# Layer one's modulation weights in 1 MB transfers, the negative maxima of four tiles in one copy, new transfer costs in the planner

## The chip, the cores and the metric

The kernel runs on one core of a Trainium2 chip. The metric is the device time of one execution in microseconds (us), lower being better; three runs of the kernel before gave a median of 1363.16 us (1362.76 to 1366.52).

The names used below: PE is TensorE, which multiplies matrices; PEld is its loading of weights; DVE is VectorE; ACT is ScalarE; POOL is GpSimd; SP is SyncE, which here issues nearly every transfer between memories (DMA). Each engine works through its own list of instructions in order, and waits at one whose inputs are not there yet.

## The reference

Two layers of a diffusion backbone over 1024 tokens of width 1024, with 256 context tokens. Each layer computes a shift, a scale and a gate from a conditioning vector (the modulation, `silu(c) @ w_mod[i] + b_mod[i]`), normalises and modulates the tokens, mixes them and adds the gated result. Layer zero's mixer is grouped-query attention (16 query heads, 4 key heads, width 64) over tokens and context; layer one's is attention in a neighbourhood of 8 rows by 16 columns plus the context.

```python
for i in range(DEPTH):
    mod_x = (silu_c @ w_mod[i] + b_mod[i])[:, None, :]
    mod_c = silu_cc @ w_mod[i] + b_mod[i]
    sh_x, sc_x, g_x = jnp.split(mod_x, 3, axis=-1)
    hx = rms_norm(x, norm_g[i]) * (1.0 + sc_x) + sh_x
    ...
    if i % N_MIXERS == 0:
        yx, yc = gqa_axial_mixer(hx, hc, ...)
    else:
        yx, yc = neighbourhood_mixer(hx, hc, ...)
    x = x + g_x * yx
return rms_norm(x, final_norm_g)
```

Inside layer zero's mixer, for each block of queries: `s = q @ k_all * scale`, `p = softmax(s)`, `o = p @ v_all`.

## The kernel before

**Tiles and stages.** The 1024 tokens are eight tiles of 128, the context two more. Matrix products run in 16-bit floats with each operand split into a high and a low part. The stages follow each other on PE: loading, normalisation and the key/value projection (to about 96 us of the trace); layer zero's attention over eight head pairs `u`, with the projections of the next pair and the modulation blocks beside it (to about 650 us); the output projection and the second normalisation (to about 810 us); layer one's attention, again eight pairs (to about 1290 us), and the last output projection.

**Layer zero's attention.** For each head pair `u` the tiles form three groups (`pt`): four tiles, four tiles, and the two of the context. `a_proj` projects queries (`pa`, L946), normalises and rotates them into `q16`, and a transposing DMA (L963) puts them into `q1`, whose lower half a copy (L965) puts into `q2`. `mgen` computes all scores once for their maximum alone: matmuls `pm` (L976) and `pmc` (L982), each followed by a maximum on DVE. `rows` reduces these maxima over a group, negates them into a 128x128 tile `zmax` (L1001), transposes that by DMA into `zt` (L1002), and copies its rows into partition 64 of `q2` (L1006, L1008), so that the product of 65 rows of `q2` and `k2` (L1184) already holds the score less its maximum. Then `a_att` forms transposed scores `st` (L1183, L1184), takes the exponential twice on ACT (`ph` L1168, `pf` L1170), splits off the low part on POOL (`pl`, L1045), and multiplies by the values (`pv`, L1051 to L1053).

For the first six pairs (`QH`) only one head of the two goes that way. The other head goes through `q_att`: scores `qs` (L1116 on `q1`, L1117 on `q2`) with queries on the partitions, a maximum on DVE (L1119), the exponentials, and transposing DMAs of 2048 columns (`qpt`, L1130; `qct`, L1139) ahead of the product with the values (`qpv`, L1104). In these pairs `q2` is `[128, 4 tiles, 2 heads, 128]`, and only head 0 of each tile gets a row of maxima: four rows apart in memory, copied one by one (L1006). In the last two pairs, and for the context, both heads get rows, in one copy (L1008).

`pm`, `pmc` and `qs` share two buffers of the matmul memory (tag `mx`), `st` has two of its own.

**The modulation blocks.** `mod_block` runs eight times within layer zero's attention: two for layer zero's gate, six for layer one. Each loads 512 columns of `w_mod` in two halves of four row tiles into `wg`, which has one buffer (L602, one 256 KB transfer per row tile), multiplies them (L610), and writes the result to memory.

**What sets the order.** The code emits work in a hand-written time line (`timeline`, by places such as `u + 0.2`). Then `Planner` takes all instructions, computes which depends on which, and simulates the five engines with `cost` (busy time, and time until the result is there), five times over with due times from the pass before; the best order it finds is fixed on each engine. For its dependencies `box` takes an access as the range from its first to its last element in each partition. For a DMA, `cost` returns the time to issue it on SP and the time that it holds the DMA engines.

Of the kernel before, what the change touches and what calls it, by code (L numbers as in the profile page):

```python
# [13 lines left out]
F16 = mybir.dt.float16  # L14
# [7 lines left out]
P = 128  # L22
D = 1024
KT = D // P
# [22 lines left out]
class Planner:  # L47
# [42 lines left out]
    def cost(self, x, rd, wr):  # L90

        k, e = type(x).__name__, self.ENG[x.engine.name]
        outs = [a for a in x.outs if hasattr(a, "bass_ap")]
        ins = [a for a in x.ins if hasattr(a, "bass_ap")]
        n = max([self.elems(a) for a in outs + ins] or [1])
        psum = any(str(getattr(a.bass_ap.tensor, "space", "")) == "PSUM" for a in ins)
        if e == "PE":
            f32 = ins[0].dtype == mybir.dt.float32
            cols = self.elems(outs[0])
            if outs[0].bass_ap.tensor.name.startswith("warm"):  # L100
                return 130.0, 170.0
            passes = (2 if x.is_transpose else 4) if f32 else 1
            if f32 and any("idf" in a.bass_ap.tensor.name for a in ins):
                passes = 2
            if not f32 and cols <= 65:
                return 30.0 if cols == 65 else 34.0, 170.0
            return max(cols * passes / 2.4 + 3.0, 29.0), 170.0
        if k == "InstDmaTransposeAnt":
            m = 1
            for s, c in list(ins[0].ap):  # L110
                m *= c
            return 1340.0, m / 128 * 23.4 / 16
        if k == "InstDMACopy":
            m = 1
            for s, c in list(outs[0].ap):
                m *= c
            run = [self.run(a) for a in (outs[0], ins[0])]
            ro = min(min(run), 1024) * 4
            return (470.0 if len(list(outs[0].ap)) < 3 else 600.0), m * 4 / ro * (11 + ro * 0.0432) / 16
        if e == "ACT":  # L120
            ptr = sum(1 for a in ins[1:] if self.elems(a) == 1)
            o = n / 1.2 + (50 if psum else 85) + (100, 100, 200)[ptr] * (ptr > 0) + (93 if len(outs) > 1 else 0)
            return o, 110.0
        if e == "DVE":
            two = len([a for a in ins if self.elems(a) > 2]) > 1
            rate = 0.96
            if not psum and not two and k in ("InstTensorCopy", "InstTensorScalarPtr"):
                rate = 3.84 if all(a.dtype != mybir.dt.float32 for a in ins + outs) else 1.92
            return n / rate + 70, 82.0
        if e == "POOL":  # L130
            if k == "InstTensorTensor":
                if getattr(x, "op", None) == mybir.AluOpType.pow:
                    return 980.0 if n > 1 else 560.0, 30.0
                return 150 + n * (1.95 if any(a.dtype != mybir.dt.float32 for a in ins) else 2.1), 40.0
            return 60 + n, 40.0
        return 50.0, 50.0
# [365 lines left out]
def trunk_kernel(ctx, tc, x, cx, cc, norm_g, ng_row, b_cols, sel_c, w_mod, w_mod0, b_mod, a_qz, a_kv, a_qg, a_kg, a_w_out,  # L502
                 b_in, rpb, b_w_out, fin_g, cos_t, sin_t, mask_q, out):
    nc = tc.nc
    V, S, G, T, DM = nc.vector, nc.scalar, nc.gpsimd, nc.tensor, nc.sync
# [6 lines left out]
    def ps_pj(name, dt=F32, shape=(P, 512)):  # L512
        return psum.tile(list(shape), dt, name=name, tag="pj", bufs=2)
# [79 lines left out]
    def mod_block(pool, l, c0):  # L593

        nm = f"{l}{c0}"
        r = c0 // D
        row = pool.tile([P, P], F32, name="mrow" + nm, tag="mrow", bufs=1)
        for hf in range(2):
            wm = pool.tile([P, KT // 2, 512], F32, name=f"wg{nm}{hf}", tag="wg", bufs=1)
            for i in range(KT // 2):  # L600
                kt = hf * KT // 2 + i
                DM.dma_start(wm[:, i], w_mod[l, kt * P:(kt + 1) * P, c0:c0 + 512])  # L602
                yield 1.0
            if hf:
                brow = com.tile([P, 512], F32, name="brow" + nm, tag="stage", bufs=4)[0:1]
                DM.dma_start(brow, b_mod[l:l + 1, c0:c0 + 512])
            ps = ps_pj(f"pmg{nm}{hf}", shape=(P, 2, P))
            for i in range(KT // 2):
                for j in range(4):
                    T.matmul(ps[32 * j:32 * j + 32, 0], s2[:, hf * KT // 2 + i, :], wm[:, i, j * P:(j + 1) * P],  # L610
                             start=i == 0, stop=not hf and i == KT // 2 - 1)
            if hf:
                for j in range(4):
                    T.matmul(ps[32 * j:32 * j + 32, 0], twos, brow[:, j * P:(j + 1) * P], start=False, stop=True)
            if not hf:
                V.tensor_copy(row, ps[:, 0])
            else:
                V.tensor_tensor(row, ps[:, 0], row, op=ALU.add)
        if r == 1:
            gr = pool.tile([P, P], F32, name="gr" + nm, tag="gr", bufs=1)  # L620
            g0 = ng_row[l:l + 1, c0 - D:c0 - D + 1]
            DM.dma_start(gr, bass.AP(g0.tensor, g0.offset, [[P, 4], [0, 32], [1, P]]))
            V.tensor_scalar(row, row, 0.5, 1.0, op0=ALU.mult, op1=ALU.add)
            V.tensor_tensor(row, row, gr, op=ALU.mult)
        else:
            V.tensor_scalar_mul(row, row, 0.5 / WS if r == 2 else 0.5)
        for v in range(2):
            dst = gate_d[l, v, c0 - 2 * D:c0 - 2 * D + 512] if r == 2 else mod_d[r, v, c0 % D:c0 % D + 512]
            DM.dma_start(dst.rearrange("(j c) -> j c", c=P), row[v:P:32])
        yield 1.0  # L630
# [292 lines left out]
    def a_proj(u, at):  # L923
# [62 lines left out]
        def rows(pts):  # L986

            zm = zmax[nrow[0] % len(zmax)]
            nrow[0] += 1
            zf = aq.tile([P, 16], F32, name=f"zf{u}{pts[0]}", tag="zf", bufs=2)  # L990
            zt = aq.tile([P, P], F16, name=f"zt{u}{pts[0]}", tag="zt", bufs=2)
            c0, outs = 0, []
            for pt_ in pts:
                mxs, n = pairs[(u, pt_)][3], PTN[pt_]
                hs = (0,) if pt_ < 2 and u in QH else (0, 1)
                zv = zf[:, c0:c0 + n * len(hs)].rearrange("p (t h) -> p t h", h=len(hs))
                for i in hs:
                    V.tensor_reduce(zv[:, :, i], mxs[i] if pt_ < 2 else mxs[i][:, 0:n, 2:3], axis=AX.X, op=ALU.max)
                outs.append((c0, n, len(hs), pairs[(u, pt_)][1]))
                c0 += n * len(hs)  # L1000
            V.tensor_scalar(zm[:, 0:c0], zf[:, 0:c0], -1.0, CSH, op0=ALU.mult, op1=ALU.add)  # L1001
            DM.dma_start_transpose(zt, zm)  # L1002
            for c, n, h, q2 in outs:
                for t in range(n) if h == 1 else (None,):
                    if h == 1:
                        DM.dma_start(q2[64:65, t, 0, :], zt[c + t:c + t + 1])  # L1006
                    else:
                        DM.dma_start(q2[64:65], zt[c:c + n * h])  # L1008
            yield 200

        items = []
        for b in range(NT // 2):
            m = (1100 if u in QH else 2200) if b < 4 else 440
            if u == 0:
                v, w, vp, vm, mw = FIRST[b]
            else:
                v = at + 0.2 * b
                w, vp, vm, mw = 0.2, v + 0.29, v + 0.31, 0.2 * m / (1100 if u in QH else 2200)
            items.append((mm(b), v, v + w, 5120))
            items.append((post(b), vp, vp + 0.01, 220))  # L1020
            items.append((mgen(b), vm, vm + mw, m))
            if b in (1, 4):
                items.append((rows((0,) if b == 1 else (1, 2)), vm + mw + 0.01, vm + mw + 0.02, 400))
# [216 lines left out]
    for n, m in enumerate(mods):  # L1240
        items.append((mod_block(aq, *m), 0.1 + 0.9 * n, 0.1 + 0.9 * (n + 1), 9.0))
# [417 lines left out]
```

## Time and profile before

| | |
|---|---|
| median of three runs | 1363.16 us (1362.76 to 1366.52) |
| profiled execution, its own time | 1365.58 us |
| its span, first to last instruction | 1363.8 us |
| granted PE clock | 0.999 |
| DMA packets, bytes | 426,959, 198.23 MB, mean 145 GB/s |
| hardware queue of SP | 426,216 packets, 195.98 MB, 65.3% of the engines' time |

A row of the profile names line, engine, operation, what is written and read (`out<-in`, buffer numbers left out), the shape and the count. Windows are in us from the start of the span. `SPq` is SP's queue, whose issuing of transfers is not counted as an engine's work. Matmuls overlap each other, and their ends are modelled.

### The profile page before, as it was taken

How to read it: one execution, taken by the hardware profiler on the slowest of the kernel's cores; microseconds unless marked ns; L12 is line 12 of the kernel's file. 1: busy time of each engine (PE TensorE's matmuls, PEld its weight loads, DVE VectorE, ACT ScalarE, POOL GpSimd, SP SyncE). 2: the span in 40 equal slices, each digit the busy share in tenths (PEclk: the TensorE clock that was granted, in tenths of full speed). 3: DMA queues.
4: the chain of work that ended last, by engine and by line, in shares of the span. 5: the costliest groups of instructions: out<-in, count | busy, mean ns of one | idle time of the engine just before them, and what ended most of it. 6: DMA issues, size and time to landing. Idle time of an engine off the chain costs nothing.

```text
span 1363.8 us, 34709 instructions
## 1 busy us (share of the span) xinstructions
PE 1329.9 (98%) x13183; PEld 927.6 (68%) x13183; DVE 1003.1 (74%) x2647; ACT 910.2 (67%) x2186; POOL 664.7 (49%) x855
## 2 busy tenths in 40 slices
PE   9999999999999999999999999999999999999897
PEld 6457777777777777776554486777768686867543
DVE  5788788878788789887276846777776867777743
ACT  3653788888787876878632437777776777786711
POOL 2573787777778775788743201312222222332332
PEclk9999999999999999999999999999999999999999
DMA  9652577878789777847066725666576656677932
GB/s 352 186 162 76 108 145 156 154 161 166 149 152 169 146 150 138 172 145 210 10 171 175 178 80 120 125 132 138 117 153 110 156 96 146 113 159 141 194 101 102
DMA packets 426959, 198.23 MB, mean 145 GB/s; under 512 B 382560, under 2 KB 389664, under 8 KB 426792
## 3 DMA queue, kind: packets, MB, share of 16 engines
q1 hardware_dynamic: 426216, 195.98, 65.3%
q8 instruction: 103, 1.69, 0.5%
q14 instruction: 64, 0.52, 0.1%
q10 hardware_dynamic: 576, 0.03, 0.0%
HBM read 90.51 MB, written 15.22 MB: 78 GB/s over the span
## 4 chain that ended last, share of the span: by engine, by line
PE 68%; DVE 11%; ACT 9%; DMA 5%; POOL 3%; issue 3%; SPq 1%; DVEq 0%; POOLq 0%; ACTq 0%
PE pa L946 11%; PE pb L1360 9%; PE pvz L1393 9%; PE poa L1275 7%; PE pob L1566 6%; PE st L1183 2%; PE st L1184 2%; PE pkv L817 2%; ACT bpf L1464 2%; PE pm L976 2%; PE bpv L1473 1%; PE pv L1052 1%; PE qpv L1104 1%; PE pv L1053 1%; PE pv L1051 1%
## 5 line engine op out<-in xcount | busy, mean ns | idle before, releaser
L1045 POOL TENSOR_TENSOR pl<-pf,ph 128x256 f16<-128x256 f32 x340 | 234.1, 714 | 58.2 <-ACT pf L1170 44.5
L1045 POOL TENSOR_TENSOR bph<-bpf,bph 128x256 f16<-128x256 f32 (+1 forms) x128 | 99.9, 790 | 319.5 <-ACT bpf L1464 256.3
L946 PE MATMUL pa<-wa,x 128*128 128x256 f16 x1536 | 213.4, 272 | 0.1
L1360 PE MATMUL pb<-hb_hi,wb 128*128 128x512 f16 (+1 forms) x640 | 193.3, 358 | 1.4 <-DVE bk L1379 1.0
L1393 PE MATMUL pvz<-wb,hb_hi 128*128 128x256 f16 x1024 | 175.4, 273 | 0.6 <-DVE bk L1379 0.3
L946 PEld LDWEIGHTS <-x 128*128 128x128 f16 x1536 | 143.2, 97 | 35.7 <-issue 1.3
L1168 ACT ACTIVATE ph<-st 128x512 f16<-128x512 f32 x200 | 119.1, 604 | 60.7 <-PE st L1184 50.0
L1360 PEld LDWEIGHTS <-wb 128*128 128x128 f16 x960 | 92.7, 98 | 72.5 <-issue 2.9
L1393 PE MATMUL pvz<-wb,hb_lo 128*128 128x256 f16 x512 | 139.6, 273 | 0.0
L1170 ACT ACTIVATE pf<-st 128x512 f32<-128x512 f32 x200 | 119.3, 609 | 1.7 <-POOL pl L1045 1.6
L977 DVE TENSOR_REDUCE mxp<-pm 128x1 f32<-128x512 f32 x160 | 107.9, 684 | 13.7 <-PE pm L976 12.3
L1045 POOL TENSOR_TENSOR qpp<-qpf,qpp 128x512 f16<-128x512 f32 x84 | 97.9, 1186 | 38.4 <-ACT qpf L1127 32.2
L1360 PE MATMUL pb<-hb_lo,wb 128*128 128x512 f16 (+1 forms) x320 | 114.4, 358 | 0.0
L1393 PEld LDWEIGHTS <-hb_hi 128*128 128x128 f16 x1024 | 97.1, 98 | 24.2 <-DVE bk L1379 1.1
L1051 PE MATMUL pv<-v,ph 128*128 128x65 f16 x800 | 104.0, 193 | 0.2 <-ACT ph L1168 0.2
L1052 PE MATMUL pv<-v,ph 128*128 128x64 f16 x800 | 104.0, 195 | 0.0
L1053 PE MATMUL pv<-v,pl 128*128 128x65 f16 x800 | 101.4, 192 | 0.5 <-POOL pl L1045 0.5
L1566 PE MATMUL pob<-wob,ob 128*128 128x512 f16 x384 | 86.7, 379 | 2.6 <-DVE bmx L1444 0.9
L1051 PEld LDWEIGHTS <-ph 128*128 128x128 f16 x800 | 75.8, 97 | 19.0 <-ACT ph L1168 0.7
L1462 ACT ACTIVATE bph<-bpf,bnx 128x384 f16<-128x384 f32 (+1 forms) x128 | 68.7, 582 | 27.2 <-DVE bnx L1454 27.1
L1052 PEld LDWEIGHTS <-ph 128*128 128x128 f16 x800 | 75.5, 97 | 12.6
L1053 PEld LDWEIGHTS <-pl 128*128 128x128 f16 x800 | 76.1, 99 | 10.5 <-POOL pl L1045 1.6
(272 smaller groups left out, 3812.1 us busy)
## 6 DMA issues: line engine op xcount, KB each, us to landing
wg<-in_w_mod SPq DMA_DIRECT2D x64, 256.0 KB
wsb<-in_b_in SPq DMA_DIRECT2D x64, 256.0 KB
wm<-in_w_mod SPq DMA_DIRECT2D x16, 512.0 KB
wsa<-in_a_qz SPq DMA_DIRECT2D x32, 256.0 KB
xstage<-in_x SPq DMA_DIRECT2D x8, 512.0 KB
wsoa<-in_a_w_out SPq DMA_DIRECT2D x16, 256.0 KB
x<-in_x SPq DMA_DIRECT2D x8, 512.0 KB
x_d<-x SPq DMA_DIRECT2D x8, 512.0 KB
```

The lines of the kernel that those rows point to most:

```text
L946: T.matmul(ps[:, :, i, :], hA(a, kt, t), wt[w][:, kt, :], start=n == 0, stop=n == 3 * KT - 1)
L977: V.tensor_reduce(mxs[i][:, t, ch:ch + 1], pm, axis=AX.X, op=ALU.max)
L1045: G.tensor_tensor(lo[:, c], p32[:, c], hi[:, c], op=ALU.subtract)
L1051: T.matmul(pv[:, t, :], hi[:, c], v[:, 0:65], start=first and t == 0, stop=False)
L1052: T.matmul(pv[:, t, 0:HD], hi[:, c], v[:, 65:129], start=False, stop=False)
L1053: T.matmul(pv[:, t, :], lo[:, c], v[:, 0:65], start=False, stop=last and t == n - 1)
L1168: S.activation(ph, st, AF.Exp)
L1170: S.activation(p32, st, AF.Exp)
L1275: T.matmul(ps, lhs(a, kt), w[b][:, kt, :], start=n == 0, stop=n == 3 * KT - 1)
L1360: T.matmul(ps[:, 0:n].rearrange("p (t q) -> p t q", q=P), wt[a][:, kt, which * P:(which + 1) * P], hb[b][:, c0 // P:(c0 + n) // P, kt], st ...
L1393: T.matmul(ps[:, :, j, :], hb[a][:, t, kt], wt[w][:, kt, 256:512], start=m == 0, stop=m == 3 * KT - 1)
L1566: T.matmul(ps, ob[kt][:, t // 4, a, c], wout["b"][hf][b][:, kt, :], start=n == 0, stop=n == 3 * KT - 1)
```

## The change

Three edits. The four loads of a `wg` half become one transfer of 1 MB, through a view of `w_mod` with the row tile as an inner dimension; the step that `timeline` counts for it is the same in sum. The copies of negative maxima become one per group for every pair: for the first six pairs it writes four places of `q2` from four rows of `zt`. And the planner's costs change: a transposing DMA of 2048 columns takes 1900 ns to issue in place of 1340, and a copy's bytes follow the type, two per element for 16-bit floats in place of four throughout, with runs counted in bytes up to 4096.

```diff
         if k == "InstDmaTransposeAnt":
 ...
-            return 1340.0, m / 128 * 23.4 / 16
+            return (1900.0 if m == 2048 * P else 1340.0), m / 128 * 23.4 / 16
         if k == "InstDMACopy":
 ...
-            ro = min(min(run), 1024) * 4
-            return (470.0 if len(list(outs[0].ap)) < 3 else 600.0), m * 4 / ro * (11 + ro * 0.0432) / 16
+            by = 2 if outs[0].dtype == F16 else 4
+            ro = min(min(run) * by, 4096)
+            return (470.0 if len(list(outs[0].ap)) < 3 else 600.0), m * by / ro * (11 + ro * 0.0432) / 16
 ...
             wm = pool.tile([P, KT // 2, 512], F32, name=f"wg{nm}{hf}", tag="wg", bufs=1)
-            for i in range(KT // 2):
-                kt = hf * KT // 2 + i
-                DM.dma_start(wm[:, i], w_mod[l, kt * P:(kt + 1) * P, c0:c0 + 512])
-                yield 1.0
+            r0 = hf * KT // 2 * P
+            DM.dma_start(wm, w_mod[l, r0:r0 + KT // 2 * P, c0:c0 + 512].rearrange("(k p) c -> p k c", p=P))
+            yield 4.0
 ...
             for c, n, h, q2 in outs:
-                for t in range(n) if h == 1 else (None,):
-                    if h == 1:
-                        DM.dma_start(q2[64:65, t, 0, :], zt[c + t:c + t + 1])
-                    else:
-                        DM.dma_start(q2[64:65], zt[c:c + n * h])
+                DM.dma_start(q2[64:65, :, 0, :] if h == 1 else q2[64:65], zt[c:c + n * h])
```

SP has 84 transfers fewer: 48 loads of `wg` and 36 row copies. No other engine has an instruction more or less, but the planner's order of all of them is new; on PE it is nearly the old one again from layer one's first projection on (282 of 9,988 rows stand elsewhere). From L603 to L1000 a line keeps its number; those after L1008 stand four lines higher in the new kernel (L1117 is L1113 there, L1184 is L1180).

First piece, PE, where the first head pair's scores begin. In the names the first digit is the pair, the second the group; `q1` and `q2` are the queries, `pm02` a tile of maxima, `qs00` the scores of `q_att`, `st00` those of `a_att`. Before:

```order
L976 LDWEIGHTS q101_1466
L976 MATMUL pm02000_1627<-k1_128,q101_1466 128x512
L1116 LDWEIGHTS q100_1314
L1116 MATMUL qs0000_1673<-k1_128,q100_1314 128x512
L1117 LDWEIGHTS q200_1315
L1117 MATMUL qs0000_1673<-k2_129,q200_1315 128x512
L1116 LDWEIGHTS q100_1314
L1116 MATMUL qs0001_1698<-k1_128,q100_1314 128x512
L1117 LDWEIGHTS q200_1315
L1117 MATMUL qs0001_1698<-k2_129,q200_1315 128x512
```

Now, at the same place, and fourteen projection matmuls later:

```order
L976 LDWEIGHTS q101_1466
L976 MATMUL pm02000_1624<-k1_128,q101_1466 128x512
L1112 LDWEIGHTS q100_1314
L1112 MATMUL qs0000_1670<-k1_128,q100_1314 128x512
L1112 LDWEIGHTS q100_1314
L1112 MATMUL qs0001_1695<-k1_128,q100_1314 128x512
```

```order
L1180 LDWEIGHTS k2_129
L1180 MATMUL st0000_1654<-q200_1315,k2_129 128x512
L1113 LDWEIGHTS q200_1315
L1113 MATMUL qs0000_1670<-k2_129,q200_1315 128x512
L1113 LDWEIGHTS q200_1315
L1113 MATMUL qs0001_1695<-k2_129,q200_1315 128x512
```

The second half of each `qs` product, which read `q2` ahead of the row copies, now stands behind the first `st` that needs them, and the two `qs` tiles stay open meanwhile.

Second piece, SP, the same group's transpose and copies (`zt00`, `q200`). Before:

```order
L963 DMA_TRANSPOSE q101_1466<-q16q02_1554 128x4x128
L965 DMA q201_1467<-q101_1466 64x512
L1002 DMA_TRANSPOSE zt00_1593<-zmax0_1303 128x128
L963 DMA_TRANSPOSE q101_1466<-q16q03_1643 128x4x128
L1006 DMA q200_1315<-zt00_1593 1x16x8 x4
L606 DMA brow02048_3006<-in_b_mod 1x512
L965 DMA q201_1467<-q101_1466 64x512
```

Now:

```order
L963 DMA_TRANSPOSE q101_1466<-q16q02_1554 128x4x128
L1002 DMA_TRANSPOSE zt00_1593<-zmax0_1303 128x128
L965 DMA q201_1467<-q101_1466 64x512
L1004 DMA q200_1315<-zt00_1593 1x4x128
L606 DMA brow02048_2991<-in_b_mod 1x512
L963 DMA_TRANSPOSE q101_1466<-q16q03_1640 128x4x128
```

Four copies are one, the transpose of the maxima has moved ahead of a copy of queries, and a transpose of queries has moved behind.

Third piece, SP, the second group of pair 3 (`zt31`, copies into `q231` and, for the context, `q232`) beside a load of modulation weights (`wg1512`, second half). Before:

```order
L1002 DMA_TRANSPOSE zt31_6319<-zmax1_1304 128x128
L1062 DMA_TRANSPOSE oa2_5295<-ol21_5987 128x8x128
L602 DMA wg15121_6368<-in_w_mod 128x512
L1006 DMA q231_5173<-zt31_6319 1x16x8 x4
L1008 DMA q232_5746<-zt31_6319 1x4x128
L965 DMA q240_6118<-q140_6117 64x512
L1087 DMA oa_d_1299<-oa2_5295 128x2048
L1130 DMA_TRANSPOSE qpt301_6291<-qpp301_6286 128x16x128
L602 DMA wg15121_6368<-in_w_mod 128x512 x3
```

Now:

```order
L1002 DMA_TRANSPOSE zt31_6277<-zmax1_1304 128x128
L963 DMA_TRANSPOSE q140_6077<-q16q40_6298 128x4x128
L873 DMA wsa61_8352<-in_a_qz 128x512
L602 DMA wg15121_6323<-in_w_mod 128x4x512
L1004 DMA q231_5140<-zt31_6277 1x4x128
L1004 DMA q232_5707<-zt31_6277 1x4x128
L1058 DMA_TRANSPOSE oa2_5261<-ol21_5947 128x8x128
```

One of the four loads stood ahead of the copies; now the whole megabyte does.

## The prediction

> **What bounds the kernel now.** I read the page's busy shares and slices first.
>
> ```profile
> span 1363.8 us, 34709 instructions
> PE 1329.9 (98%) x13183; PEld 927.6 (68%) x13183; DVE 1003.1 (74%) x2647; ACT 910.2 (67%) x2186; POOL 664.7 (49%) x855
> PEclk9999999999999999999999999999999999999999
> GB/s 352 186 162 76 108 145 156 154 161 166 149 152 169 146 150 138 172 145 210 10 171 175 178 80 120 125 132 138 117 153 110 156 96 146 113 159 141 194 101 102
> ```
>
> TensorE (PE) is busy 98% of the span at full clock; 1363.8 - 1329.9 leaves 33.9 us idle. The change takes no matmul away, so it can only move waits. Next, the windows view by stage (the columns are the stretch, its length, then busy time and instruction count of each engine, clock, share of the DMA engines, GB/s).
>
> ```profile
> 0.00:96.00 96.00, 90.92 (x624) 52.17 (x625) 72.62 (x160) 52.53 (x105) 49.49 (x77) 1.00 0.72 241
> 96.00:650.00 554.00, 543.09 (x6786) 412.33 (x6784) 456.39 (x1238) 423.17 (x874) 402.08 (x511) 1.00 0.73 149
> 810.00:1210.00 400.00, 398.86 (x3672) 292.62 (x3670) 292.79 (x853) 294.83 (x860) 98.62 (x138) 1.00 0.65 130
> 1210.00:1290.00 80.00, 72.69 (x682) 51.80 (x681) 60.49 (x185) 63.47 (x195) 28.41 (x35) 1.00 0.79 156
> ```
>
> The edited lines run in the second row, layer zero's attention: idle there 554.0 - 543.1 = 10.9 us. What ended that idle time is the waits view of PE for this stretch (the longest of its rows; total, times, longest):
>
> ```profile
> PE st L1184 <- DMA q<-zt: 3.4, 3, 2.5
> PE st L1183 <- ACT pf L1170: 1.6, 4, 0.7
> PE qs L1116 <- DVE mxp L977: 1.3, 3, 0.5
> PE pmc L982 <- DVE mxp L977: 0.7, 2, 0.5
> PE pm L976 <- DMA q<-q16q: 0.7, 2, 0.5
> PE qpv L1104 <- DMA qpt<-qpp: 0.6, 1, 0.6
> PE qs L1116 <- DVE qmx L1119: 0.6, 2, 0.4
> PE pm L976 <- DVE mxp L977: 0.5, 2, 0.3
> ```
>
> DMA waits are 3.4 + 0.7 + 0.6 = 4.7 us, waits for VectorE (DVE) about 4.2 us with the smaller rows, the rest ScalarE and POOL. No row names `wg`, the modulation weights: PE never waits for the transfers that the first edit merges. The idle column hides a little: a 512-wide matmul is drawn 0.38 us long but the next starts 0.22 us after it (rows further down), so each wait costs some 0.16 us more than it shows.
>
> **What the edits take off SyncE's queue.** This is one line's view each (duration in ns: min/median/max):
>
> ```profile
> L602 SPq DMA_DIRECT2D wg<-in_w_mod x64: 327/454/1955, 102.9 to 618.6; - x64
> L1006 SPq DMA_DIRECT2D q<-zt x48: 506/587/1556, 127.5 to 501.4; - x48
> L1008 SPq DMA_DIRECT2D q<-zt x12: 605/662/729, 157.7 to 648.1; - x12
> L1130 SPq DMA_TRANSPOSE qpt<-qpp x48: 1511/1900/4736, 139.1 to 557.0; - x48
> SPq L1130 <- POOL pl L1045: 47.9, 22, 5.0
> ```
>
> Row copies: 48 x 0.587 = 28.2 us become 12 x 0.662 = 7.9 us (L1008 has the merged form already), so 20 us less issuing. Weights: 64 x 0.454 = 29.1 us become 16 issues of a 1 MB form that no row has; the nearest are one 256 KB issue at its shortest, 0.33 us, and four of them at the median, 1.8 us; I take 0.6, nearer the single one, since most of a row's length beyond 0.33 us is the queue's state, so 9.6 us and 19 us less. The 39 us come out of a queue that in this stretch waits for POOL 47.9 us in its first row alone: **off the path, worth 0 by themselves**. What shortens is a chain: the fourth row copy is issued 3 x 0.587 = 1.76 us after the first, and `st` needs all four. The planner's new 1.90 us for a 2048-column transpose is the median of L1130, so its plan fits these 60 instructions better; that too acts only through the order.
>
> **The chain of the negative maxima in the new order.** The last maximum matmul (`pm`, `pmc`), DVE's reductions, the transpose `zt`, the copies into row 64 of `q2`, then `st`. For the first head pair, from the timelines of PE and SyncE:
>
> ```profile
> 121.40 0.38 PE L982 MATMUL pmc<-k,q 128*128 128x256 f16 x2
> 121.61 0.27 PE L946 MATMUL pa<-wa,xc_hi 128*128 128x256 f16 x1
> 123.77 1.15 SPq L1002 DMA_TRANSPOSE zt<-zmax  x1
> 127.46 2.49 SPq L1006 DMA_DIRECT2D q<-zt  x4
> 131.25 0.60 PE L1184 MATMUL st<-q,k 65*128 65x512 f16 x2
> ```
>
> From the end of `pmc` (121.8, where DVE can start) to the transpose 2.0 us, to the copies 3.7, and `st` came at 131.25 without a wait. For the last pair, and another place where a copy was waited for (timeline of PE, chain of waits):
>
> ```profile
> 634.95 0.60 PE L982 MATMUL pmc<-k,q 128*128 128x256 f16 x4
> 635.54 0.19 PE L1053 MATMUL pv<-v,pl 128*128 128x65 f16 x1
> 635.57 0.19 PE L1051 MATMUL pv<-v,ph 128*128 128x65 f16 x1
> 639.79 7.53 DMA zt<-zmax
> 647.34 3.37 DMA q<-zt
> 650.75 0.39 PE st L1184
> 327.89 1.73 DMA q<-zt
> 350.83 0.38 PE L982 MATMUL pmc<-k,q 128*128 128x256 f16 x2
> 354.77 1.18 SPq L1002 DMA_TRANSPOSE zt<-zmax  x1
> ```
>
> (the last two rows, of the timelines, are those of pair 3's second half)
>
> A copy lands 1.73 to 3.4 us after its issue begins. With one copy the chain is at the least 2.0 + 3.7 + 1.7 = 7.4 us, up to 9.1 with the slow landing. Now the order: between the last maximum and the first `st` of that tile group stand matmuls of 0.109 us (256 wide), 0.216 us (512 wide) and 0.03 us (64 or 65 wide; starts in the rows above and below). First pair: before 61 of 256 and 10 of 512, 8.8 us; now 47 and 4, 6.0 us. The planner took the saved time and more. So PE waits 1.4 to 3.1 us here, I take 1.7. The same count gives 13.2 to 9.1 us for pair 2's second half and 13.7 to 8.2 for pair 5's: 0 to 0.9 each, I take 0.4. For pair 3's second half, 13.0 to 11.9, the 1 MB load now stands between the transpose and the copy (third order piece): 0.75 MB more ahead at the first slice's 352 GB/s is 2.2 us, and 3.6 (from 351.2 to 354.8 above) + 3.7 + 3.4 + 2.2 = 12.9 against 11.9; 0.7. Last pair: 12.7 to 10.8 us, where PE already waited 2.5 us; its chain keeps one copy as before, but in SyncE's new order 0.75 MB less of loads stands between the last `q16q` transpose and `zt`, 2.2 us: 15.1 - 2.2 - 10.8 = 2.1, or 4.3 without that; 2.9. Sum 1.7 + 0.4 + 0.4 + 0.7 + 2.9 = 6.1 for 3.4 now: **+2.7 us**, bounds -1 and +6.
>
> There is an added wait in it. A merged copy's range, from its first element to its last, covers the other head's columns of three of the four tiles, so in the plan `q_att`'s L1117, which reads only that head, is put behind the copy. The first order piece shows it for pair 0. For the other pairs `qs` stood behind `st` anyway, so it costs nothing there.
>
> **DVE's buffers.** PE's score tiles `pm`, `pmc`, `qs` alternate over two buffers, each freed by one DVE pass:
>
> ```profile
> L977 DVE TENSOR_REDUCE mxp<-pm x160: 658/681/693, 114.0 to 626.6; 128x1 f32<-128x512 f32 x160
> 124.34 0.38 PE L1116 MATMUL qs<-k,q 128*128 128x512 f16 x1
> 124.56 0.38 PE L1117 MATMUL qs<-k,q 65*128 65x512 f16 x1
> 125.29 0.38 PE L1116 MATMUL qs<-k,q 128*128 128x512 f16 x1 [0.35 <-DVE mxp L977]
> ```
>
> Where less than one pass (0.68 us) of PE work lies between a buffer's last write and its next, PE must wait. By the durations above the order of before has 21 such places among 376 tiles, the new one 11; under 0.9 us it is 33 and 20. DVE's 4.2 us and 0.16 us hidden in each of its 13 waits make 6.3 us; in proportion 20/33 of it stays: **-2.5 us**, bounds -6 and +1.
>
> **The rest.** `q<-q16q` and `qpt` waits (1.3 us): a freer queue issues them earlier, **-0.6**, bounds -1.3 and +1.5. Start: the new order loads `wm` ahead of `xstage`. Both are needed for the first `pkv`, the first slice is full at 352 GB/s, and what follows has the same sequence: 0, bounds -1 and +1. From the first `pb` matmul on, PE's order is the same but for 282 of 9,988 places: 0.
>
> Sum +2.7 - 2.5 - 0.6 = **-0.4 us**. The profiled execution took 1365.58 us (span 1363.8 and 1.8 around it), 2.4 above the median of 1363.16: 1365.2 for it, **1362.8 us** as a median.
>
> **The rivals.** *Faster*: the looser order and the freer queue count fully. Then DVE's 6.3 us halve and more (-4), 4.7 us of DMA waits go to 1 (-3.7), giving 1355.5 us; for it speaks that all tight places get fewer, against it that `st` moved nearer to its copy. The Trainium skill ("DMA: Bandwidth & Descriptors", Bandwidth) tells to batch transfers to 1 MiB or more; by the 2.0 us it gives as the fixed part of one DMA, 48 fewer would be an estimated 96 us of DMA time. By that rule this rival should be the likely one; the trace does not agree that it is time of the kernel, as no wait of PE names `wg`. *Slower*: a 1 MB load is a plug. Everything that SyncE issues behind it queues behind it, as the last `zt` took 7.53 us where the first pair's took 3.7. In the new order nine of the 16 loads have a `qpt` transpose within two rows behind them; before, most had three pieces, 768 KB, there. 256 KB more is 0.75 us at 352 GB/s and 1.8 at the stage's 149, so up to 9 x 1.8 = 16, and half of it if half meet slack: 8 us, less 1 for the other terms, 1370. It decides once `qpt`'s slack falls under 1.8 us; the one 0.6 us wait says that slack is small but there. The skill's same page (Queues, rings and completion order) has an engine consume descriptors in ring order, which is this mechanism. That the 39 us saved on SyncE stay idle is the forecast itself.
>
> **Chances.** Forecast 0.58 (own range 1359 to 1367), faster rival 0.24, plug 0.13, a dearer `zt` chain alone (+6) 0.05. About 0.3% (4.1 us) is what can be told from no change: faster 0.25, within 0.57, slower 0.18. Low end 1356, near the faster rival; high end 1369.5, near the plug.
>
> **What would show it.** In the new profile: idle of PE in 96 to 650 us still 8 to 14 us; `st <- DMA q<-zt` up from 3.4 to 5 or 6 us, most of it at the first and last pair; DVE rows down to about 2.5 us; no wait on `wg`; the same idle from 810 us on. A PE order that runs far from its plan, with many `qpt` waits, would prove me wrong, as would a start that differs by over 2 us.

## The result, and the profile after

The new kernel takes **1368.31 us** (median of 12 runs, 1366.6 to 1373.82), the old one 1364.12 us beside it: ratio 1.0034, 95% interval 1.002 to 1.0049. A second series of 11 runs gave 1.0023 (1.0011 to 1.0035). So it is slower by about 0.3%, not the 0.4 us faster that was forecast.

The profiled execution took 1367.65 us, 2.1 us more than the old one's 1365.58. That pair shows less than the medians do, since the old one's execution lay 1.5 us above its median and the new one's 0.7 us below. The page of the new kernel, and its windows by stage (columns as before):

```profile
span 1365.9 us, 34575 instructions
PE 1332.4 (98%) x13183; PEld 928.3 (68%) x13183; DVE 1002.0 (73%) x2647; ACT 910.0 (67%) x2186; POOL 668.2 (49%) x855
```

```profile
56.00:66.00 10.00, 9.17 (x44) 5.07 (x45) 9.42 (x24) 7.89 (x18) 9.31 (x14) 0.83 0.35 50
96.00:650.00 554.00, 543.38 (x6770) 412.79 (x6768) 458.13 (x1239) 423.49 (x876) 401.24 (x508) 1.00 0.70 149
810.00:1210.00 400.00, 398.75 (x3665) 292.49 (x3664) 290.27 (x851) 292.24 (x854) 98.69 (x137) 1.00 0.63 128
1210.00:1290.00 80.00, 73.35 (x696) 52.98 (x695) 61.08 (x183) 63.97 (x197) 26.19 (x33) 1.00 0.79 157
```

PE's idle time in 96 to 650 us is 10.6 us, as before (10.9), and from 810 us on little moved (398.86 and 72.69 us of PE's work in the last two windows before). The clock of 0.83 in the first row is new. To find the stage that lost, look at three marks in PE's timelines: the first and the last `pkv`, between which the key/value projection lies, and the first `pb`, with which layer one begins. Old kernel, then new:

```profile
18.53 2.75 PE L817 MATMUL pkv<-wkv,x 128*128 128x512 f16 x12
94.67 0.38 PE L817 MATMUL pkv<-wkv,xc_lo 128*128 128x512 f16 x1
765.99 0.38 PE L1360 MATMUL pb<-hb_hi,wb 128*128 128x512 f16 x1
```

```profile
19.25 2.75 PE L817 MATMUL pkv<-wkv,x 128*128 128x512 f16 x12
97.09 0.38 PE L817 MATMUL pkv<-wkv,xc_lo 128*128 128x512 f16 x1
768.40 0.38 PE L1356 MATMUL pb<-hb_hi,wb 128*128 128x512 f16 x1
```

All of this pair's loss, 97.09 - 94.67 = 2.4 us, lies in the start. Of it, 0.7 us is there at the first `pkv` already (19.25 and 18.53 us); from the first to the last `pkv` the old kernel took 76.1 us and the new one 77.8. From the last `pkv` to the first `pb`, where the edited lines run, both took 671.3 us, and behind that 597.8 and 597.5 us. Yet the attention's waits are not the same ones. The new kernel's waits of PE in 96 to 655 us:

```profile
PE st L1180 <- DMA q<-zt: 2.3, 2, 2.0
PE qs L1112 <- DVE mxp L977: 1.9, 2, 1.6
PE st L1179 <- ACT pf L1166: 1.8, 4, 0.7
PE qs L1112 <- DVE qmx L1115: 1.2, 4, 0.5
PE pm L976 <- DVE qmx L1115: 0.8, 2, 0.7
PE qpv L1100 <- DMA qpt<-qpp: 0.7, 1, 0.7
PE pa L946 <- DVE mrow L616: 0.7, 2, 0.4
```

The copies' row fell from 3.4 to 2.3 us, and the rows of DVE, with the smaller ones, rose from 4.2 to 5.6 (in the second series' trace 2.0 and 5.9).

**What happens at the start.** PE's timeline around 55 us, new kernel, and then the old one's row at the same place:

```profile
53.13 0.89 PE L807 MATMUL pl<-idf,xstage 128*128 128x128 f32 x4 [0.61 <-ACT tf L809]
56.83 0.59 PE L817 MATMUL pkv<-wkv,x 128*128 128x512 f16 x2 [2.81 <-POOL x L812]
57.26 0.40 PE L807 MATMUL pl<-idf,xstage 128*128 128x128 f32 x2
57.48 0.61 PE L817 MATMUL pkv<-wkv,x 128*128 128x512 f16 x1
57.88 0.64 PE L807 MATMUL pl<-idf,xstage 128*128 128x128 f32 x2
58.31 3.18 PE L817 MATMUL pkv<-wkv,x 128*128 128x512 f16 x8
```

```profile
54.87 1.46 PE L817 MATMUL pkv<-wkv,x 128*128 128x512 f16 x6 [1.30 <-DVE t2k L748]
```

PE waits 2.81 us in place of 1.30, and the eight `pkv` behind it take 3.18 us, at half clock. The timelines of DVE and POOL at that place, new kernel (the row of `t1k` at 55.60 us left out):

```profile
53.57 1.58 DVE L800 TENSOR_SCALAR xstage<-xstage,rs_ln 128x1024 f32<-128x1024 f32 x2 [0.72 <-POOL rs_ln L637]
55.06 0.62 DVE L813 TENSOR_TENSOR x<-tf,x 128x256 f16<-128x256 f32 x1
55.94 0.41 DVE L813 TENSOR_TENSOR x<-tf,x 128x256 f16<-128x256 f32 x1
56.27 0.41 DVE L748 TENSOR_TENSOR t2k<-pkv,gsk 128x256 f32<-128x256 f32 x1
54.01 1.39 POOL L812 CAST x<-tf 128x256 f16<-128x256 f32 x2
56.40 0.40 POOL L812 CAST x<-tf 128x256 f16<-128x256 f32 x1 [0.99 <-ACT tf L809]
```

In the old kernel's DVE timeline one `L800` and one `L813` stand ahead of `t2k`:

```profile
52.85 0.76 DVE L800 TENSOR_SCALAR xstage<-xstage,rs_ln 128x1024 f32<-128x1024 f32 x1 [0.73 <-POOL rs_ln L637]
53.52 0.42 DVE L748 TENSOR_TENSOR t1k<-pkv,gck 128x256 f32<-128x256 f32 x1
53.89 0.58 DVE L813 TENSOR_TENSOR x<-tf,x 128x256 f16<-128x256 f32 x1
54.40 0.41 DVE L748 TENSOR_TENSOR t2k<-pkv,gsk 128x256 f32<-128x256 f32 x1
```

The new row puts PE's wait down to POOL's copy, which ended last, at 56.80 us. But the `pkv` that waits reads only the first of the two copies at 54.01 us. It belongs to tile 4 and takes over the buffer of tile 0's `pkv` (`ps_kv`: tag `st`, two buffers), and the program makes it wait for the last reader of that buffer, DVE's `t2k`, as the old kernel's row says. `t2k` ends at 56.68 us in place of 54.81. The new plan puts a second scaling of tokens (`L800`) and a second `L813` ahead of it: from the first `L800` to `t2k` DVE takes 2.70 us (53.57 to 56.27) in place of 1.55 (52.85 to 54.40). That is 1.15 us; the other 0.7 us of the delay is what PE and DVE were behind already. No edited line is part of this: the planner ordered it anew. The place is read from the trace; no run moves these two rows alone.

### The profile page after: what moved, and what is told of

It reads as the page before. It is cut to its first block, busy times and chain, and to the rows that moved or that the text cites. A ratio compares the mean times of both kernels' runs of the same rounds, so it can differ in the third digit from the quotient of the medians.

```text
span 1365.9 us, 34575 instructions
## 1 busy us (share of the span) xinstructions
PE 1332.4 (98%) x13183; PEld 928.3 (68%) x13183; DVE 1002.0 (73%) x2647; ACT 910.0 (67%) x2186; POOL 668.2 (49%) x855
## 4 chain that ended last, share of the span: by engine, by line
PE 71%; DVE 10%; ACT 10%; DMA 3%; issue 3%; POOL 2%; SPq 0%; DVEq 0%; POOLq 0%; ACTq 0%
PE pa L946 11%; PE pb L1356 10%; PE pvz L1389 9%; PE poa L1271 7%; PE pob L1562 5%; PE st L1179 2%; PE st L1180 2%; PE pm L976 2%; ACT bpf L1460 2%; PE pv L1048 2%; PE bpv L1469 2%; PE pv L1047 1%; PE pv L1049 1%; PE pvz L1392 1%; PE qs L1112 1%
## 5 line engine op out<-in xcount | busy, mean ns | idle before, releaser
L1049 PE MATMUL pv<-v,pl 128*128 128x65 f16 x800 | 104.5, 192 | 0.0
```

The costliest lines, as they stand in the source:

```text
L1049: T.matmul(pv[:, t, :], lo[:, c], v[:, 0:65], start=False, stop=last and t == n - 1)
```

## The experiments

Theory 1: the new order of the start is the loss. Its rivals: the 1 MB loads (2), the merged copies (3), the new order of the attention (4). Theory 5, a sum of several of these, was formed after the first eight runs.

In every run but 5 an order worked out beforehand is put in place of the planner's own, so that one thing changes at a time:

```diff
-        plan.schedule(margin=100.0)
-        plan.refine(5, 100.0, 300.0)
+        plan.order = fixed_order()
         plan.apply()
```

`fixed_order` returns a written-out list for each engine. "Start" means all instructions that the program emits ahead of the first `pa`. Where a transfer is split or merged in a fixed order, the pieces stand at the place of the one, and the one at the place of the first piece. Every ratio is to the old kernel, measured beside it; the medians are of 11 or 12 executions, of five in run 4 and of seven in run 17.

| run | start | order behind it | loads | copies | ratio (95%) | last `pkv`, us | to first `pb`, us |
|---|---|---|---|---|---|---|---|
| old kernel | old | old | 4 | 4 | 1 | 94.67 | 671.3 |
| new kernel | new | new | 1 | 1 | 1.0034 (1.002, 1.0049) | 97.09 | 671.3 |
| 5, new again | new | new | 1 | 1 | 1.0023 (1.0011, 1.0035) | 97.21 | 670.7 |
| 1 | old | new | 1 | 1 | 1.0009 (0.9998, 1.0019) | 94.89 | 671.2 |
| 2 | new | old | 4 | 4 | 1.0018 (1.0008, 1.0028) | 97.25 | 670.1 |
| 3 | new | new | 4 | 1 | 1.0022 (1.0011, 1.0033) | 96.75 | 668.9 |
| 4 | new | new | 1 | 4 | 1.0063 (1.005, 1.0076) | 96.70 | 676.5 |
| 6, gap filled | new | new | 1 | 1 | 1.0015 (1.0006, 1.0024) | 96.74 | 671.7 |
| 7 | old | old | 4 | 1 | 0.9974 (0.9963, 0.9985) | 94.57 | 667.2 |
| 8 | old | new | 4 | 1 | 1.0006 (0.9997, 1.0016) | 95.66 | 670.6 |
| 9 | old | old | 1 | 1 | 0.9993 (0.998, 1.0006) | 94.84 | 667.3 |

The last two columns are of each run's one trace, read as above, and a traced execution can lie some us beside its run's median.

**The start.** Run 1 gives the new kernel the old start, run 2 the old kernel the new one.

> The new kernel with its own planned order on all engines, except that the instructions of the loading, normalisation and key/value stage (all that the program emits ahead of the first query projection) stand as in the old kernel. Theory 1 (the loss is the new order of the start: first transposes 0.7 us later and a 2.8 us wait of PE at 56.8 us with half clock behind it): the last pa of the first group starts 2.4 us earlier than in the new kernel's trace (at 121.9 in place of 124.3 us), idle of PE in 0 to 96 us falls by 2 us, and the time is 1364.5 to 1366.0 us, ratio to the old kernel 1.000 to 1.0015. Theory 2 (the 1 MB loads), theory 3 (the merged row copies) and theory 4 (the new order of layer zero's attention): the start gains at most 1 us that the attention gives back, ratio 1.0025 to 1.0045 as for the new kernel.

> The reverse: the old kernel with its own order and its own transfers, but the instructions of the loading, normalisation and key/value stage in the new kernel's order. Theory 1: slower than the old kernel by 2 to 4 us, ratio 1.0015 to 1.003, with the 2 to 3 us wait of PE near 57 us. Theories 2, 3 and 4: no loss beyond 1 us, ratio 0.9995 to 1.001.

> The new kernel once more, beside the next three, so that they can be compared without another chip between them. Theory 1 (the start's order costs 2.4 us, the rest little): ratio to the old kernel 1.002 to 1.004, last pa of the first group 2.4 us later than in the old kernel. If the ratio is again 1.0034 or above, 1.5 us or more of the loss lies behind the start.

The start's order carries its loss with it wherever it is put. From the first to the last `pkv` all six traces with the new start took 77.8 us, and the fourteen with the old start (those of the table further down too) 76.1 to 76.6: the order costs about 1.7 us. The other 0.7 us of the first pair is not shown to be the order's, since the first `pkv` comes at 18.0 to 19.6 us in the traces with the old start and at 18.9 to 19.4 with the new. In times the loss is 0.0018 (2.5 us) in run 2, and 0.0014 to 0.0025 from run 1 to the two series of the new kernel. Theory 1 holds for the start. Run 1 keeps about 0.0009 over the old kernel, which its interval does not tell from nothing; whether something lies behind the start is for the runs on the copies.

**The half clock.** Run 6 adds matmuls on constants where PE waits; their result is not used.

```diff
-    warm_up(100)
+    warm_up(100); fill = ps_mx("fill"); [T.matmul(fill[:, 0:2 * P], wone[:, 0:P], wone, start=True, stop=True) for _ in range(24)]
```

> The new kernel's order, with 24 more matmuls of 256 columns (about 0.11 us each, on constants, their result is not read) on PE ahead of the first pkv of tile 4, where PE waits 2.8 us. The inputs of that pkv come at the same time as before. Theory 1a (the wait puts PE at half clock for the next 3.4 us, which costs 1.7 us by itself): no wait over 0.5 us there, the pkv behind it 216 ns apart in place of 426, granted clock 1.00 in 56 to 66 us in place of 0.83, and 1.2 to 1.7 us less than the new kernel. Theory 1b (the slow stretch comes from the operands or from another engine, not from the idle): the same 426 ns, no gain, or up to 0.5 us lost.

PE's timeline of run 6, and its window from 56 to 66 us:

```profile
53.51 2.78 PE L853 MATMUL fill<-wone 128*128 128x256 f16 x24
56.47 0.59 PE L817 MATMUL pkv<-wkv,x 128*128 128x512 f16 x2 [0.18 <-POOL x L812]
56.90 0.38 PE L807 MATMUL pl<-idf,xstage 128*128 128x128 f32 x2
57.12 0.38 PE L817 MATMUL pkv<-wkv,x 128*128 128x512 f16 x1
57.33 0.38 PE L807 MATMUL pl<-idf,xstage 128*128 128x128 f32 x2
57.55 1.89 PE L817 MATMUL pkv<-wkv,x 128*128 128x512 f16 x8
```

```profile
56.00:66.00 10.00, 9.68 (x56) 5.00 (x55) 9.42 (x23) 8.20 (x18) 9.67 (x14) 1.00 0.31 47
```

The mechanism of 1a is shown: the eight `pkv` take 1.89 us in place of 3.18, at full clock. Its price is a miss: run 6's first `pkv` comes at 18.90 us and its last at 96.74, which is 77.8 us, no less than without the filling, and 1.0015 beside 1.0023 cannot be told apart. Behind the eight `pkv` PE is 2.05 us ahead of the new kernel's trace (57.55 + 1.89 beside 58.31 + 3.18), of which 0.35 us was there at the first `pkv`; at the last one it is 0.35 again, so all that the filling gained is lost in between. The half clock is a symptom; the order of the other engines is what costs.

**The 1 MB loads and the copies.** Each edit is undone by itself in the new order (runs 3 and 4), and the copies alone are put into the old order (run 7).

```diff
-            r0 = hf * KT // 2 * P
-            DM.dma_start(wm, w_mod[l, r0:r0 + KT // 2 * P, c0:c0 + 512].rearrange("(k p) c -> p k c", p=P))
-            yield 4.0
+            for i in range(KT // 2):
+                kt = hf * KT // 2 + i
+                DM.dma_start(wm[:, i], w_mod[l, kt * P:(kt + 1) * P, c0:c0 + 512])
+                yield 1.0
```

This is run 3's edit for the loads; run 4 takes the copies' edit back in the same way.

> The new kernel with its whole order fixed, but each 1 MB load of wg again four transfers of 256 KB, one behind the other at the place of the one. Theories 1, 3 and 4: as the new kernel, ratio 1.0025 to 1.0045 (48 more issues on SyncE of 0.45 us, in a queue that waits for others). Theory 2 (the 1 MB form itself delays what queues behind it, or splits badly over the engines): 1364 to 1366 us, ratio 1.000 to 1.0015.

> The new kernel's order behind the start, merged copies, but the old kernel's order of the start and four loads of 256 KB in place of each 1 MB one. Theory 1: 2.4 us under the new kernel, about the old kernel's time, ratio 0.9995 to 1.0012. If the 1 MB form costs as well (the runs with four loads stood 1.7 us below the new kernel's first 12, but within their interval): 0.9980 to 0.9997.

> The new kernel with its whole order fixed, but each merged copy of four rows of maxima again four copies, one behind the other at the place of the one. Theories 1, 2 and 4: three more issues of 0.59 us lie in the chain ahead of st, 1.8 us at the first pair, where st follows its maxima by 6.0 us of matmuls, and up to 1 us each at two others: 1369.5 to 1371.5 us, ratio 1.0035 to 1.0055. Theory 3 (the merged copy is itself dearer than the four, by its form or by the wait that its range brings): 1365 to 1367 us, ratio 1.0005 to 1.002.

> The old kernel's order and its four loads, with only the copies of maxima merged, each at the place of the first of its four; the two qs of the first pair that the planner had put behind the copy stay ahead of it. If the chip needed that order, PE would wait for the copy at qs L1113 near 126 us, some 4 us. If only the planner's range of the copy asks for it: no such wait, the st <- q<-zt row falls from 3.4 to 2.5 us or less (the last pair keeps its one copy), and the time is 0 to 1.5 us under the old kernel, ratio 0.9988 to 1.0.

> The new kernel's transfers (1 MB loads, merged copies) in the old kernel's order on all engines, each merged transfer at the place of the first of its four. It differs from the new kernel in nothing but the order. Theory 5 (the merged copy by itself is worth 3 to 4 us, the loads nothing, and the planner's new orders of start and attention cost 2.4 and 4 to 5 us): ratio 0.9965 to 0.9985 as for the merged copies alone (0.9974). Theory 2 (a 1 MB load is a plug for what is issued behind it, which the new order had moved out of the way): 0.9985 to 1.001.

In the new order the size of the loads changes nothing: 1.0022 for 1.0023, and with the old start 1.0006 for 1.0009. In the old order, whose rows were not planned for it, the 1 MB form went from 0.9974 to 0.9993, 2.6 us whose intervals overlap (0.9985 and 0.998). In run 9's trace there is a wait that run 7's lacks altogether:

```profile
PE st L1179 <- DMA q<-zt: 2.3, 2, 1.3
```

That would be theory 2's plug, as run 9's expectation has it, a third of the size that its rival had; overlapping intervals and one trace of each do not settle it. The merged copy is worth 0.0026, 3.6 us, in the old order, and 0.003 to 0.004 (4 to 5.5 us, run 4 beside the new kernel's two series) in the new one; theory 3 falls. Both are more than I expected (at most 0.0012 in the old order, and 1.0055 for run 4). Run 7's trace has no wait of `qs` at 126 us for the copy, so the dependency that the range added exists only in the plan. Its largest rows:

```profile
PE st L1179 <- ACT pf L1166: 2.1, 5, 0.7
PE qpv L1100 <- DMA qpt<-qpp: 1.8, 2, 1.0
PE qs L1112 <- DVE qmx L1115: 1.0, 4, 0.4
```

So the transfers of the new kernel, in the old order, are not slower than the old kernel (run 9), and the order is what turned them into a loss: the start 0.0014 to 0.0025, and the attention 0.0032 with four loads (run 7 to run 8, intervals far apart). With the 1 MB loads the attention's step is 0.0016 (run 9 to run 1), and there the intervals overlap.

**Why the new order of the attention is worse.** All of these have the old start, merged copies and 1 MB loads (run 12 apart, which has the old transfers), and differ in what the planner was told. Runs 10, 17 and 18 give the planner the merged copy as four pieces:

```diff
-            wr = [b for b in map(self.box, x.outs) if b]
+            wr = [b for a in x.outs for b in self.parts(x, a) if b]
```

The function `parts`, which the edit adds, is left out here. Run 13 keeps of the new prices only the 1900 ns, run 14 only the price of the bytes, runs 11 and 18 neither. Runs 15 and 16 take their order from a second plan, drawn with another constant:

```diff
-        plan.refine(5, 100.0, 300.0)
+        plan.refine(5, 100.0, 310.0)
```

| run | 1900 ns | bytes | four pieces | ratio (95%) | to first `pb`, us |
|---|---|---|---|---|---|
| 1 | yes | yes | no | 1.0009 (0.9998, 1.0019) | 671.2 |
| 10 | yes | yes | yes | 1.0004 (0.9992, 1.0017) | 669.5 |
| 16, second draw | yes | yes | no | 1.0017 (1.0001, 1.0032) | 666.3 |
| 14 | no | yes | no | 0.9985 (0.997, 1.0001) | 667.4 |
| 11 | no | no | no | 0.9969 (0.9959, 0.9979) | 663.2 |
| 15, second draw | no | no | no | 0.9985 (0.9973, 0.9998) | 667.2 |
| 18 | no | no | yes | 0.9977 (0.9967, 0.9987) | 666.0 |
| 13 | yes | no | no | 0.9969 (0.9955, 0.9983) | 665.3 |
| 17 | yes | no | yes | 0.9964 (0.995, 0.9977) | 665.1 |
| 12, old transfers | yes | yes | no | 0.9992 (0.9981, 1.0003) | 665.3 |

(Run 16's traced execution took 1361.03 us where its median is 1366.42, so its last column flatters it; those of runs 11 and 12 lie 2.5 us under their medians.)

> The new kernel planned anew, with the merged copy entered into the planner as its four pieces in place of one range from first to last element, so that the first pair's qs are no longer put behind it; start as in the old kernel. To be set beside the new order with the old start (1.0009). Theory 5a (the added dependency is what makes the new attention order bad: the 1.6 us wait of qs for a maximum near 128 us goes, and what follows from it): 0.9970 to 0.9990. Theory 5b (it is the planner's use of the shorter chain, st moved nearer to its copy, whatever the range): 1.0000 to 1.0020, st <- q<-zt still 2 us or more.

> The new kernel's transfers, planned with the old costs, start as in the old kernel. To be set beside the new order with the old start (1.0009). Theory 5c (the planner's new costs make the attention order bad): 0.9970 to 0.9990. Theory 5b (the shorter chain alone is enough): 1.0000 to 1.0020.

> The old kernel's transfers, planned with the new costs, start as in the old kernel: the third edit alone, without its effect on the start. Theory 5c (the new costs are the cause): 1.0020 to 1.0040. Theory 5b (the shorter chain is the cause, and here there is none): 0.9990 to 1.0010. A change of 1.0020 or more here without 5c holding in the run with old costs would say that any new plan of the attention comes out some us away from the old one.

> The new transfers, start as in the old kernel, planned with the old costs but for the 1900 ns of a 2048-column transpose. Theory 5d (it is the new price of a copy's bytes that makes the attention order bad: where it is in the plan, PE has some 17.5 us of other work between the last pair's last maximum and its st, in place of 20 to 21): as with the old costs, 0.9960 to 0.9985, no st <- q<-zt wait at 640 to 655 us. Theory 5e (the two new prices together, or the transposes' price): 0.9995 to 1.0015. Theory 5f (each plan is a draw that scatters by some us whatever the prices): anywhere from 0.996 to 1.002.

> The same with the new price of a copy's bytes alone, and the old 1340 ns for every transpose. Theory 5d: 0.9990 to 1.0015, with a wait st <- q<-zt of 1 to 2 us at 640 to 655 us. Theory 5e: 0.9960 to 0.9985. Theory 5f: anywhere from 0.996 to 1.002.

> The new transfers, planned with the old costs as in the run of 0.9969, start as in the old kernel, but with 310 in place of 300 ns in the due times that the planner hands from pass to pass: a change that means nothing, for a second draw of the order. Theories 5d and 5e (the new prices are the cause): 0.9960 to 0.9985 again. Theory 5f (a draw): may be 0.999 to 1.002.

> The same second draw with the new costs, to be set beside 1.0009 (new order, old start). Theories 5d and 5e: 1.0000 to 1.0020 again. Theory 5f: may be 0.996 to 0.999. From the fifth pair on this draw's distances between maxima and st are those of the new kernel, so a time of 1.0009 says less of the second half than of the first.

> The new transfers and old start, planned with the 1900 ns for the transposes, the old price of a copy's bytes, and the merged copy entered as its four pieces. To be set beside the same plan without the pieces (0.9969), where qs waits 1.6 us for a maximum near 128 us. If that wait costs what it shows: gone, and 0.9950 to 0.9965. If its time is given back behind it: 0.9965 to 0.9985.

> The same with the old price of a transpose as well: only the merged copy's four pieces are new in the planner. To be set beside the old costs without the pieces (0.9969 and 0.9985 in two draws). If the new prices, both in the plan, are what spoils it (0.9969 to 0.9985 in four plans with one or none of them, 1.0004 to 1.0017 in three with both): at or under 0.9985. If plans only scatter: it may be 0.999 or above, and the grouping by prices falls.

Plans of the new transfers fall into two groups: 0.9964 to 0.9985 in six with one or none of the new prices, 1.0004 to 1.0017 in three with both. The range is not the cause (run 10), the shorter chain is not (run 11), and 1900 ns alone does no harm (run 13). The price of the bytes alone sits at the upper edge of the good group (run 14). The intervals of runs 11, 13, 17 and 18 lie wholly below those of all three; those of runs 14 and 15 reach into run 10's. Two draws with the same prices differ by 0.0016 (runs 11 and 15, whose intervals overlap a little), half of the step between the groups. Two cautions: the three plans with both prices share their distances from last maximum to `st` from the fifth pair on, so they are not three independent draws; and the run with the old transfers and both prices (0.9992) lost nothing, where theory 5c expected 1.0020 or more, so the prices are not a cause by themselves. That both prices together gave these transfers a worse plan is shown for these plans; why they do is open.

Where in the attention it shows is open. In 300 to 500 us PE's waits sum to 3.7 us in the new kernel's trace, in many short ones for every engine, and to 1.0 in run 11's; but they sum to 3.5 us in run 18, of the good group, and to 2.7 in run 10, of the other.

Run 17 has a miss: I expected the wait of `qs` near 128 us to go with the range, but at 125.98 us it still stood there,

```profile
125.98 0.38 PE L1118 MATMUL qs<-k,q 128*128 128x512 f16 x1 [1.40 <-DVE mxp L983]
```

so that wait does not come from the range. That it comes from how `pm` and `qs` follow each other is likely, but not shown.

**The best version.** Run 17 (new transfers, old start, only the 1900 ns as a new price, four pieces) takes 1358.15 us beside 1362.65: ratio 0.9964, faster than both kernels. Runs 11 and 13 cannot be told apart from it, nor can run 7 (0.9974), the old order with nothing but the merged copies.

## Why the prediction was wrong

**The failed step is "Start".** It said: both loads are needed for the first `pkv`, "what follows has the same sequence: 0, bounds -1 and +1". What follows did not have the same sequence: on DVE a second `L800` and a second `L813` had moved ahead of the `t2k` that frees the buffer of tile 4's `pkv`. From the first to the last `pkv` the new order costs 1.7 us in every trace, and run 2 lost 2.5 us by it. The first half of the sentence, on the loads, is not refuted: the first `pkv` came 0.7 us later in the pair of traces, but within what the old start's traces scatter by (18.0 to 19.6 us). I looked at SyncE's first rows and never set the orders of DVE, ACT and POOL ahead of 96 us side by side, where 98% busy says that any wait of PE counts. The text's own test, a start that differs by over 2 us, is what came in the pair of traces.

The start alone does not make up the miss. Between 1362.8 and 1368.31 us lie 5.5 us: 1.0 is the old kernel's own median (1364.12 beside the new one, 1363.16 before), 1.7 to 2.5 the start, and some 2 to 3 us are left. They are not in the pair of traces, and the second series has 1.5 us less of them (1.0023 for 1.0034). What runs 7 and 8 show in their place is that the new order of the attention gave back the gain of the merged copies.

**The chain of maxima**, +2.7 us, had the wrong sign: its row fell by 1.1 us. At the last pair PE waited 2.0 of the 2.9 us forecast; at the first, where 1.7 were forecast, it waited for DVE at `qs`, and then no longer for the copy at `st`:

```profile
128.76 0.38 PE L1112 MATMUL qs<-k,q 128*128 128x512 f16 x1 [1.61 <-DVE mxp L977]
130.61 0.38 PE L1180 MATMUL st<-q,k 65*128 65x512 f16 x1
```

I let the count of matmuls between maximum and `st` decide and took the slow landings with it. Run 4 shows the copies' worth at these distances: three issues more at each place, and 4 to 5.5 us in sum. In the old order the same gain was there to be kept, 3.6 us.

**DVE's buffers**, -2.5 us, had the wrong sign too: from 4.2 to 5.6 us, where 2.5 was forecast. The count of tight places (21 to 11) did not measure these waits. That they arise where DVE comes late, which a count of PE's work does not see, is my reading.

**The other waits for DMA**, -0.6 us: from 1.3 to 1.1 us (0.7 of `qpt`, the rest `qct`), within its bounds. **Second half**, 0: right (597.8 and 597.5 us).

So the attention came out near its forecast, 671.3 us before and after in the pair of traces, but by luck: two errors cancel. In the runs it is a gain of 3.6 us by the merged copy, taken back by the order.

**The rivals.** The plug was priced at 8 us; it is nothing in the new order. The faster rival was right that the shorter chain is worth some 4 us (1355.5 forecast; the best plan took 1358.15 beside 1362.65), wrong in taking the new order for the looser one. The Trainium skill's rule to batch transfers to 1 MiB or more ("DMA: Bandwidth & Descriptors", Bandwidth), which would have favoured it by the loads, finds nothing here: 48 transfers fewer moved 1.0022 to 1.0023. What paid was four small copies on a chain made into one. A plan as the bound, with transfers that are harmless, was no rival of mine at all.

## What to carry to other kernels

Where a planner or scheduler orders everything anew, measure an edit in the old order first (here 0.9974 for the copies), and compare the orders of all engines in every stage, also where no edited line runs. A better price in a planner's model is not a better plan: draw several and time them, since two plans of the same program came out at 0.9969 and 0.9985, and one good start can be kept while the rest is planned again.

## What the runs showed of the hardware

After the wait of 2.8 us PE ran at half clock for about 3.4 us (the eight `pkv` of the row above start 0.43 us apart, in run 6 0.22), in all five traces of kernels with the new start and an unfilled gap; in a window of 10 us that shows as a clock of 0.83, on the page's 40 slices not at all. The length of the wait does not decide it alone. The old start's wait of 1.3 us at the same place was followed by half clock in two of its fourteen traces (runs 14 and 17: a clock of 0.72 in 54 to 60 us) and by full clock in the others, and the last pair's wait of 2.5 us in the old kernel by full clock. The Trainium skill ("TensorE: Matmul & The Clock Gate", Part 1) puts the gate's return to half clock after an idle window of about 3.4 us; here it followed waits of 2.8 and of 1.3 us, with some matmuls ahead of them. And 1.3 us of slower matmuls, on the engine that is busy 98% of the time, cost nothing in the end: with and without them the first to the last `pkv` takes 77.8 us. What was gained was lost again behind them; in 66 to 96 us of the new kernel's trace DVE is busy for 27.6 of the 30 us and POOL for 27.0.
